# PEER experts' two rows in one table row: one 8 KB gather for each pick, product and sum in one pass

## The chip, the cores and the metric

The kernel runs on one core of a Trainium2 chip. The metric is the device time of one execution in microseconds (us). The engines are named as in the profile: PE (TensorE), DVE (VectorE), ACT (ScalarE), POOL (GpSimd) and SP (the queue that issues plain transfers).

## The reference

One decoder block on 1024 tokens of width 1024, in float32: a mixer (attention over a sliding window, a short convolution, a projection), a layer norm, and then a channel mixer with 16,384 experts of one neuron each, on which the change bears:

```python
v1, i1 = lax.top_k(s1, 16)            # 8 heads, two halves of a product key
v2, i2 = lax.top_k(s2, 16)
cand = v1[..., :, None] + v2[..., None, :]
sc, pos = lax.top_k(cand, 16)         # 16 experts for each head
e = i1[pos // 16] * 128 + i2[pos % 16]
g = softmax(sc)
# 8 * 16 = 128 picks for each token
u = u_experts[e]; v = v_experts[e]    # rows of 1024 floats
a = gelu(einsum('tkd,td->tk', u, x))
out = einsum('tk,tkd->td', g * a, v)
```

The block ends with `layer_norm(ALPHA * h + out)`.

## The kernel before

The 1024 tokens are eight blocks of 128, a block's tokens on the 128 partitions. The channel mixer is computed in two ways. For blocks 2 to 5 (`DENSE`) every expert is computed by matmuls: `up` (L677 to L690) loads 128 experts' u rows, splits them into two float32r parts (`uh` on ACT, `ul` on DVE, L120 and L121), multiplies on PE (L684), applies Gelu and the gates (`ge`, L689 and L690) and splits the result (`Wh`, `Wl`); `down` loads the v rows, splits them (`vh` on ACT, `vl` on POOL), multiplies (L716) and adds into `accT` on DVE (L722). There are 128 calls of each: the 256 units of the dense stage. For blocks 0, 1, 6 and 7 (`ROWS`) the rows of the picked experts are gathered: `gathered` (L139) makes 128 steps over the u table and then 128 over the v table. A u step issues an indirect DMA on POOL (L148), 128 rows of 4 KB into a tile `row`, and DVE multiplies it by the tokens' rows and sums along the row (L150). After 128 of them one Gelu (L152) and one product with the gates (L153) give the weights `a`. A v step gathers (L160), and DVE adds `row * a[:, k]` to the accumulator `acc` (L162). The tokens' rows (`h1p`) and the accumulator lie in the one PSUM tile `pg`, in turn; the gathered rows, the copies of the tokens' rows and the parameters of the second norm share five 4 KB slots (`t4k`, `NGATHER = 5`).

The steps come out of one generator. `advance_rows` takes three of them (one from `c = 26` on) behind each projection of the first stage, and `advance` (L749) takes as many behind each dense unit as brings all 1024 to their end at nine tenths of the 256 units:

```python
goal = min(total, early + AHEAD + (total - early - AHEAD) * u * 10 // (9 * units))
for _ in range(goal - done):
    step()
```

The order in which each engine gets its instructions is not the program's: a planner simulates the timeline when the kernel is built and puts an instruction into its engine's queue when its operands and its buffer are ready by its estimate. Each queue then runs in that order.

The first stage goes through the tokens in four groups of two blocks: projections (`project`, L370), attention, convolution, output projection, norm, keys and the choice of experts. A generator `side` runs the choice of the preceding group beside it; for dense blocks it also builds the gates (`gates_of_all`, L261 to L275). The tiles `x`, `y` and `h` of 8 KB share the tag `T`, with four buffers.

Of the kernel before, what the change touches and what calls it, by code (L numbers as in the profile page):

```python
# [13 lines left out]
F32 = mybir.dt.float32  # L14
# [40 lines left out]
NGATHER = 5  # L55
TK = 4
# [21 lines left out]
def block_kernel(ctx: ExitStack, tc: tile.TileContext, d, out):  # L78
# [49 lines left out]

    def second_norm(tb, src):
        par = []  # L130
        for i in (2, 3):
            p = gp.tile([P, D], F32, name="ln2", tag="t4k", bufs=NGATHER)
            G.dma_start(p, ln2d[:, i:i + 1].to_broadcast([P, 1, D]).rearrange("p a e -> p (a e)"))
            par.append(p)
        o = gp.tile([P, D], F32, name="o", tag="t4k", bufs=NGATHER)
        layer_norm(o, src, par, gp)
        G.dma_start(out[tb * P:(tb + 1) * P], o)

    def gathered(tb):  # L139
        g = gw[tb].rearrange("p h k -> p (h k)")  # L140
        h1 = gp.tile([P, D], F32, name="h1", tag="t4k", bufs=NGATHER)
        G.dma_start(h1, h1d[tb])
        h1p = pg.tile([P, D], F32, name="pg")
        act(h1p, h1, AF.Copy)
        a = gp.tile([P, P], F32, name="a", bufs=2)
        for k in range(P):
            row = gp.tile([P, D], F32, name="row", tag="t4k", bufs=NGATHER)
            G.indirect_dma_start(out=row, out_offset=None, in_=d["u"],  # L148
                                 in_offset=bass.IndirectOffsetOnAxis(ap=idx[tb][:, k:k + 1], axis=0))
            V.scalar_tensor_tensor(row, row, 1.0, h1p, op0=ALU.mult, op1=ALU.mult, accum_out=a[:, k:k + 1])  # L150
            yield True
        act(a, a, AF.Gelu)  # L152
        V.tensor_tensor(a, a, g, op=ALU.mult)  # L153
        acc = pg.tile([P, D], F32, name="pg")
        h1 = gp.tile([P, D], F32, name="h1", tag="t4k", bufs=NGATHER)
        G.dma_start(h1, h1d[tb])
        act(acc, h1, AF.Copy, scale=ALPHA)
        for k in range(P):
            row = gp.tile([P, D], F32, name="row", tag="t4k", bufs=NGATHER)
            G.indirect_dma_start(out=row, out_offset=None, in_=d["v"],  # L160
                                 in_offset=bass.IndirectOffsetOnAxis(ap=idx[tb][:, k:k + 1], axis=0))
            V.scalar_tensor_tensor(acc, row, a[:, k:k + 1], acc, op0=ALU.mult, op1=ALU.add)  # L162
            yield True
# [616 lines left out]
def lay_out(i):  # L780
    def m(name):
        return np.asarray(i[name])
# [32 lines left out]
```

## Time and profile before

| | |
|---|---|
| Time of three runs, median (lowest to highest) | 2746.32 us (2743.99 to 2756.95) |
| The profiled execution | 2743.4 us, span 2741.6 us |
| Busy: PE, DVE, ACT, POOL | 84%, 84%, 29%, 52% |
| Gathers | 1024 indirect DMAs from POOL |
| Moved | 862.21 MB, 314 GB/s over the span |

The span is the time from the first instruction to the last; the 1.8 us between it and the execution's time lie around it. A share of busy time is a mean over stages that differ: the first stage runs to about 1225 us, the dense stage to about 2612 us, and what is left runs to the end. Which engine a stage waits for is read from that stage alone.

### The profile page before, as it was taken

The page shows a single profiled execution, that of the slowest core. Times are in us where ns is not written, and L with a number is a line of the kernel's source. Part 1 is how long each engine was busy: PE and PEld are TensorE (multiplying, and loading weights), DVE is VectorE, ACT ScalarE, POOL GpSimd, SP SyncE. Part 2 cuts the span into 40 slices and gives each one's busy share as a digit, 9 for nine tenths or more (in the row PEclk, how much of TensorE's full clock was granted, in tenths as well). Part 3 has the DMA queues.
Part 4 walks back from the last instruction along what each step waited for, and adds up shares of the span by engine and source line. Part 5 has one row for each costly group of instructions (what it writes and reads, how often), then busy time and mean ns, then how long its engine had stood idle before and what let it go on. Part 6 is the DMA issues. An engine that isn't in the chain of part 4 may idle for free. (4 is left out here: it accounts for less than half of the span.)

```text
span 2741.6 us, 33269 instructions
## 1 busy us (share of the span) xinstructions
PE 2290.9 (84%) x11032; PEld 1917.8 (70%) x11032; DVE 2303.3 (84%) x4956; ACT 798.1 (29%) x1307; POOL 1415.2 (52%) x1233
## 2 busy tenths in 40 slices
PE   8999699789887622219999999999999999999940
PEld 7888587678766522218888888888888888888830
DVE  2158889999999999978888888888888888888897
ACT  2123122242443323224232322323232332323201
POOL 1000533443353344436667676666767666666753
PEclk9899799799977755559999999999999999999975
DMA  6355999899979788899999999999999999999987
GB/s 203 99 155 175 347 376 332 311 336 354 337 286 337 253 317 293 309 337 322 343 337 340 336 352 350 341 351 335 342 354 334 347 344 346 339 342 353 335 314 263
DMA packets 293900, 862.21 MB, mean 314 GB/s; under 512 B 25824, under 2 KB 97760, under 8 KB 289504
## 3 DMA queue, kind: packets, MB, share of 16 engines
q0 software_dynamic: 150480, 548.47, 54.5%
q1 hardware_dynamic: 143248, 311.62, 33.1%
q8 instruction: 87, 1.43, 0.2%
q14 instruction: 85, 0.70, 0.1%
HBM read 815.95 MB, written 44.04 MB: 314 GB/s over the span
## 5 line engine op out<-in xcount | busy, mean ns | idle before, releaser
L148 POOL DMA_INDIRECT row<-in_u,ix x512 | 532.9, 1041 | 586.7 <-DVE row L150 242.9
L160 POOL DMA_INDIRECT row<-in_v,ix x512 | 554.8, 1084 | 474.4 <-DVE pg L162 229.9
L162 DVE SCALAR_TENSOR_TENSOR pg<-row,a,pg 128x1024 f32<-128x1024 f32 x512 | 656.4, 1282 | 33.8 <-DMA row<-in_v,ix 27.8
L684 PE MATMUL pd<-hT,uh 128*128 128x512 f32 x2048 | 635.8, 390 | 42.8 <-ACT uh L120 42.8
L150 DVE SCALAR_TENSOR_TENSOR row<-row,pg 128x1024 f32<-128x1024 f32 x512 | 611.7, 1212 | 45.4 <-DMA row<-in_u,ix 44.8
L684 PEld LDWEIGHTS pd<-hT,uh 128*128 128x128 f32 x2048 | 385.4, 188 | 123.0 <-ACT uh L120 43.0
L716 PE MATMUL pd<-Wl,vh 128*128 128x512 f32 (+1 forms) x1056 | 402.3, 383 | 0.0
L684 PE MATMUL pd<-hT,ul 128*128 128x512 f32 x1024 | 399.3, 390 | 0.0
L716 PE MATMUL pd<-Wh,vh 128*128 128x512 f32 (+1 forms) x1056 | 397.4, 383 | 0.2 <-ACT Wh L120 0.2
L716 PE MATMUL pd<-Wh,vl 128*128 128x512 f32 (+1 forms) x1056 | 392.1, 383 | 0.3 <-POOL vl L121 0.3
L121 POOL TENSOR_TENSOR vl<-vraw,vh 128x1024 fp32r<-128x1024 f32 x128 | 309.4, 2417 | 72.7 <-ACT vh L120 68.6
L267 PE MATMUL pk<-o,oh 128*128 128x128 f16 x512 | 109.2, 277 | 208.2 <-DVE oh L261 131.3
L370 PE MATMUL mm<-x,raw 128*128 128x256 f32 x1152 | 269.2, 386 | 13.1 <-DMA x<-in_xT 7.7
L120 ACT ACTIVATE vh<-vraw 128x1024 fp32r<-128x1024 f32 x128 | 135.9, 1062 | 455.7 <-PE pd L716 302.1
L722 DVE TENSOR_TENSOR accT<-accT,pd 128x512 f32<-128x512 f32 (+1 forms) x256 | 169.4, 667 | 109.8 <-PE pd L716 97.8
L370 PEld LDWEIGHTS mm<-x,raw 128*128 128x128 f32 x1152 | 215.8, 193 | 45.2 <-issue 8.1
L370 PE MATMUL mm<-h,raw 128*128 128x256 f32 x1024 | 238.1, 385 | 1.5 <-ACT h L539 1.0
L716 PEld LDWEIGHTS pd<-Wh,vl 128*128 128x128 f32 x1056 | 198.4, 188 | 39.3 <-POOL vl L121 0.7
L716 PEld LDWEIGHTS pd<-Wl,vh 128*128 128x128 f32 x1056 | 198.5, 188 | 38.9 <-DVE Wl L121 0.2
L716 PEld LDWEIGHTS pd<-Wh,vh 128*128 128x128 f32 x1056 | 198.0, 188 | 39.2 <-ACT Wh L120 0.4
L121 DVE TENSOR_TENSOR ul<-uraw,uh 128x1024 fp32r<-128x1024 f32 x128 | 159.7, 1248 | 76.1 <-ACT uh L120 70.8
L684 PEld LDWEIGHTS pd<-hT,ul 128*128 128x128 f32 x1024 | 192.8, 188 | 40.9 <-DVE ul L121 0.8
(211 smaller groups left out, 2756.0 us busy)
## 6 DMA issues: line engine op xcount, KB each, us to landing
raw<-in_wall SPq DMA_DIRECT2D x168, 512.0 KB
uraw<-in_uT SPq DMA_DIRECT2D x128, 512.0 KB
vraw<-in_vL SPq DMA_DIRECT2D x128, 512.0 KB
gd<-st SPq DMA_DIRECT2D x32, 1024.0 KB
gq<-gd SPq DMA_DIRECT2D x32, 1024.0 KB
row<-in_u,ix POOLq DMA_INDIRECT x512
row<-in_v,ix POOLq DMA_INDIRECT x512
x<-in_xT SPq DMA_DIRECT2D x16, 256.0 KB
```

The lines of the kernel that those rows point to most:

```text
L120: act(dh, src, AF.Copy)
L121: eng.tensor_tensor(dl, src, dh.bitcast(F32), op=ALU.subtract)
L148: G.indirect_dma_start(out=row, out_offset=None, in_=d["u"], in_offset=bass.IndirectOffsetOnAxis(ap=idx[tb][:, k:k + 1], axis=0))
L150: V.scalar_tensor_tensor(row, row, 1.0, h1p, op0=ALU.mult, op1=ALU.mult, accum_out=a[:, k:k + 1])
L160: G.indirect_dma_start(out=row, out_offset=None, in_=d["v"], in_offset=bass.IndirectOffsetOnAxis(ap=idx[tb][:, k:k + 1], axis=0))
L162: V.scalar_tensor_tensor(acc, row, a[:, k:k + 1], acc, op0=ALU.mult, op1=ALU.add)
L267: nc.tensor.matmul(ps[:, t], oh[:, :, t2 + t], o1[:, t2 + t], start=True, stop=False)
L370: nc.tensor.matmul(ps[:, :n], w[:, j], mov[:, j, :n], start=(j == 0), stop=(j == NJ - 1))
L684: nc.tensor.matmul(ps, w[:, j], hT[z][:, j], start=(j == 0 and k == 0), stop=(j == NJ - 1 and k == 2))
L716: nc.tensor.matmul(ps, vv[:, j % 2, k], w[:, t0:t0 + n], start=(k == 0 and p == 0), stop=(k == QUAD - 1 and p == 2))
L722: V.tensor_tensor(o, o, ps, op=ALU.add)
```

## The change

The host puts the u row and the v row of an expert side by side into one table `uv`, so that a row has 8 KB. `gathered` makes one gather for each pick into a pair tile `[P, 2, D]`, of which there are five (tag `uv`). DVE forms the product of pick k in the first half; two ACT instructions on one column of `a` apply Gelu and the gate; behind the product of pick k stands the sum of pick k - 1, from the second half of its pair. The number of steps is still 1024. The tokens' rows stay in SBUF (`h1`, a tile of its own) and are an operand of the product from there; `pg` holds the accumulator alone. The second norm takes its two parameters with one DMA into a pair. Room is made by three buffers instead of four for the tag `T`, and by setting `dynamic_dma_scratch_size` to 8192.

```diff
 NGATHER = 5
+SCRATCH = 8192
...
+    def pair(name):
+        return gp.tile([P, 2, D], F32, name=name, tag="uv", bufs=NGATHER)
+
     def second_norm(tb, src):
-        par = []
-        for i in (2, 3):
-            p = gp.tile([P, D], F32, name="ln2", tag="t4k", bufs=NGATHER)
-            G.dma_start(p, ln2d[:, i:i + 1].to_broadcast([P, 1, D]).rearrange("p a e -> p (a e)"))
-            par.append(p)
-        o = gp.tile([P, D], F32, name="o", tag="t4k", bufs=NGATHER)
-        layer_norm(o, src, par, gp)
+        par = pair("ln2")
+        G.dma_start(par, ln2d[:, 2:4].to_broadcast([P, 2, D]))
+        o = pair("o")[:, 0]
+        layer_norm(o, src, (par[:, 0], par[:, 1]), gp)
         G.dma_start(out[tb * P:(tb + 1) * P], o)
 
     def gathered(tb):
...
-        h1 = gp.tile([P, D], F32, name="h1", tag="t4k", bufs=NGATHER)
+        h1 = gp.tile([P, D], F32, name="h1")
         G.dma_start(h1, h1d[tb])
-        h1p = pg.tile([P, D], F32, name="pg")
-        act(h1p, h1, AF.Copy)
+        acc = pg.tile([P, D], F32, name="pg")
+        act(acc, h1, AF.Copy, scale=ALPHA)
         a = gp.tile([P, P], F32, name="a", bufs=2)
-        for k in range(P):
-            row = gp.tile([P, D], F32, name="row", tag="t4k", bufs=NGATHER)
-            G.indirect_dma_start(out=row, out_offset=None, in_=d["u"],
-                                 in_offset=bass.IndirectOffsetOnAxis(ap=idx[tb][:, k:k + 1], axis=0))
-            V.scalar_tensor_tensor(row, row, 1.0, h1p, op0=ALU.mult, op1=ALU.mult, accum_out=a[:, k:k + 1])
-            yield True
-        act(a, a, AF.Gelu)
-        V.tensor_tensor(a, a, g, op=ALU.mult)
-        acc = pg.tile([P, D], F32, name="pg")
-        h1 = gp.tile([P, D], F32, name="h1", tag="t4k", bufs=NGATHER)
-        G.dma_start(h1, h1d[tb])
-        act(acc, h1, AF.Copy, scale=ALPHA)
-        for k in range(P):
-            row = gp.tile([P, D], F32, name="row", tag="t4k", bufs=NGATHER)
-            G.indirect_dma_start(out=row, out_offset=None, in_=d["v"],
-                                 in_offset=bass.IndirectOffsetOnAxis(ap=idx[tb][:, k:k + 1], axis=0))
-            V.scalar_tensor_tensor(acc, row, a[:, k:k + 1], acc, op0=ALU.mult, op1=ALU.add)
-            yield True
+        rows = {}
+        for k in range(P + 1):
+            if k < P:
+                rows[k] = pair("row")
+                G.indirect_dma_start(out=rows[k].rearrange("p a e -> p (a e)"), out_offset=None, in_=d["uv"],
+                                     in_offset=bass.IndirectOffsetOnAxis(ap=idx[tb][:, k:k + 1], axis=0))
+                ru = rows[k][:, 0]
+                V.scalar_tensor_tensor(ru, ru, 1.0, h1, op0=ALU.mult, op1=ALU.mult, accum_out=a[:, k:k + 1])
+                act(a[:, k:k + 1], a[:, k:k + 1], AF.Gelu)
+                act(a[:, k:k + 1], a[:, k:k + 1], AF.Copy, scale=g[:, k:k + 1])
+                yield True
+            if k:
+                V.scalar_tensor_tensor(acc, rows.pop(k - 1)[:, 1], a[:, k - 1:k], acc, op0=ALU.mult, op1=ALU.add)
+                yield True
         second_norm(tb, acc)
...
-            x = p2.tile([P, NJ, NM], F32, name="x", tag="T", bufs=4)
+            x = p2.tile([P, NJ, NM], F32, name="x", tag="T", bufs=3)
...
-        "u": f(m("u_experts")[0]),
-        "v": f(m("v_experts")[0]),
+        "uv": f(np.concatenate([m("u_experts")[0], m("v_experts")[0]], axis=1)),
...
-    nc = bacc.Bacc("TRN2", target_bir_lowering=False, num_devices=1)
+    nc = bacc.Bacc("TRN2", target_bir_lowering=False, num_devices=1, dynamic_dma_scratch_size=SCRATCH)
```

The tiles `h` and `y` get `bufs=3` likewise, and the last norm's parameters come from `pair("ln2")[:, 0]`.

## Rows read from the trace of the kernel before

**Rows 1.** The page's span in 40 equal slices, busy tenths, two of its lines

```profile
PE   8999699789887622219999999999999999999940
...
DMA  6355999899979788899999999999999999999987
```

**Rows 2.** Windows: stretch, length, PE, PEld, DVE, ACT, POOL busy; PEclk, DMA share, GB/s

```profile
300.00:400.00 100.00, 93.52 (x455) 82.00 (x454) 83.02 (x252) 20.04 (x44) 45.04 (x48) 0.91 1.00 381
...
1225.00:2612.50 1387.50, 1381.34 (x6107) 1143.80 (x6108) 1173.41 (x1474) 433.07 (x540) 936.11 (x712) 1.00 0.95 342
300.00:1225.00 925.00, 620.37 (x3438) 524.75 (x3436) 873.28 (x2631) 282.64 (x567) 394.57 (x378) 0.77 0.89 323
```

**Rows 3.** Windows of the products (L150) alone, then of the sums (L162) alone, DVE busy

```profile
0.00:1225.00 1225.00, 308.09 (x512) 0.81 0.80 286
1225.00:2612.50 1387.50, 306.79 (x512) 1.00 0.95 342
...
1225.00:2612.50 1387.50, 408.32 (x318) 1.00 0.95 342
2612.50:2715.00 102.50, 82.18 (x64) 0.61 0.92 324
```

**Rows 4.** DVE's waits from 1225 to 2612.5: total us, times, longest

```profile
DVE accT L722 <- PE pd L716: 97.6, 127, 2.2
DVE ul L121 <- ACT uh L120: 70.8, 71, 9.0
...
DVE ge L690 <- ACT ge L689: 0.8, 2, 0.5
```

**Rows 5.** DVE's waits from 300 to 1225, the longest first

```profile
DVE row L150 <- DMA row<-in_u,ix: 32.6, 37, 3.0
...
DVE a L153 <- ACT a L152: 0.4, 1, 0.4
```

**Rows 6.** The page's costliest groups of instructions: the two gathers on POOL

```profile
L148 POOL DMA_INDIRECT row<-in_u,ix x512 | 532.9, 1041 | 586.7 <-DVE row L150 242.9
L160 POOL DMA_INDIRECT row<-in_v,ix x512 | 554.8, 1084 | 474.4 <-DVE pg L162 229.9
```

**Rows 7.** The page's DMA queues: packets, MB, packets' time as share of 16 engines

```profile
q0 software_dynamic: 150480, 548.47, 54.5%
q1 hardware_dynamic: 143248, 311.62, 33.1%
```

**Rows 8.** Timeline of DVE, 1643 to 1646: start us, us, instruction

```profile
1643.20 1.23 DVE L121 TENSOR_TENSOR ul<-uraw,uh 128x1024 fp32r<-128x1024 f32 x1 [1.87 <-ACT uh L120]
1644.34 1.22 DVE L150 SCALAR_TENSOR_TENSOR row<-row,pg 128x1024 f32<-128x1024 f32 x1
1645.48 0.08 DVE L150 DVE_READ_ACCUMULATOR row<-row,pg 128x1 f32 x1
```

**Rows 9.** ACT's groups by form: small activations and table loads

```profile
L109 ACT ACT_TABLE_LOAD x8 | 10.3, 1283 | 0.1
L109 ACT ACTIVATE lnst<-lnst 128x1 f32<-128x1 f32 x16 | 3.0, 200 | 4.0 <-DVE lnst L108 3.9
...
L452 ACT ACTIVATE S<-sp,nm 128x128 f32<-128x128 f32 x8 | 2.8, 366 | 2.6 <-DVE nm L448 2.6
```

**Rows 10.** Timeline of DVE and POOL from 2600 to 2604

```profile
2600.84 2.41 POOL L121 TENSOR_TENSOR vl<-vraw,vh 128x1024 fp32r<-128x1024 f32 x1
...
2601.13 2.69 DVE L690 TENSOR_TENSOR ge<-ge,gq 128x512 f32<-128x512 f32 x1
```

**Rows 11.** Groups by form from 1225 to 2612: the splits and the gating

```profile
L121 POOL TENSOR_TENSOR vl<-vraw,vh 128x1024 fp32r<-128x1024 f32 x128 | 309.4, 2417 | 72.7 <-ACT vh L120 68.6 <-issue 2.7
...
L121 DVE TENSOR_TENSOR ul<-uraw,uh 128x1024 fp32r<-128x1024 f32 x128 | 159.7, 1248 | 76.1 <-ACT uh L120 70.8 <-issue 3.0 <-PE pd L684 1.8
...
L690 DVE TENSOR_TENSOR ge<-ge,gq 128x512 f32<-128x512 f32 x128 | 92.0, 718 | 0.8 <-ACT ge L689 0.8
```

**Rows 12.** ACT's waits from 1260 to 2600, two of the longest

```profile
ACT vh L120 <- PE pd L716: 302.1, 91, 6.6
...
ACT vh L120 <- DMA vraw<-in_vL: 108.4, 20, 8.7
```

More of the change, by code (lines that the diff above doesn't have):

```diff
@@ L530, in normed @@
             blocks, nb, n, t0 = spans(gi)
-            h_ = p2.tile([P, NJ, NM], F32, name="h", tag="T", bufs=4)
+            h_ = p2.tile([P, NJ, NM], F32, name="h", tag="T", bufs=3)
             for b, tb in enumerate(blocks):
@@ L639, in block_kernel @@
             x, qkv = xin
-            y = p2.tile([P, NJ, NM], F32, name="y", tag="T", bufs=4)
+            y = p2.tile([P, NJ, NM], F32, name="y", tag="T", bufs=3)
             for b in range(2):
@@ L769, in block_kernel @@
         for i in (2, 3):
-            p = gp.tile([P, D], F32, name="ln2", tag="t4k", bufs=NGATHER)
+            p = pair("ln2")[:, 0]
             nc.sync.dma_start(p, ln2d[:, i:i + 1].to_broadcast([P, 1, D]).rearrange("p a e -> p (a e)"))
```

## The prediction

> **What bounds the kernel now.** I read the page's slices first, to cut the span into stages, then windows of each stage, the waits of DVE and ACT in each, and the timeline where one stage hands over to the next. In the slices the reader is to see three stretches [rows 1]: PE and DMA uneven in the first 18 slices, both at nine tenths or more in the next 20, and in the last two PE gone and DMA still at work.
>
> From 300 to 1225 us DVE is busy 873 of 925 us, and PE 620 [rows 2]: here every us of DVE counts, and so does every wait of it. The largest of those is that of the products for their gather, 32.6 us in 37 waits [rows 5]; in the 100 us behind 300, where the steps come three behind each projection, the DMA share is 1.00 at 381 GB/s [rows 2].
>
> From 1225 to 2612.5 us PE is busy 1381 of 1387.5 us at full clock [rows 2], so this stage can't get shorter by anything done to the gathers. DVE has 1387.5 - 1173.4 = 214 us idle, most of it behind PE and ACT [rows 4], and the DMA share is 0.95 at 342 GB/s.
>
> At 2612.5 us PE has nothing of weight left, but 64 sums of the last block are still to come, and they take until 2715 us: 1.60 us each, of which DVE works 1.28, with the DMA engines busy 0.92 of the time [rows 3]. This tail of 102.5 us and the last norms behind it are on the path. By 1225 us 256 products and 130 sums are done; 256 products and 382 sums follow [rows 3]. So the kernel is worth what stage one's DVE, and the tail, are worth.
>
> **The change, part by part.** *Gathers.* 512 of 1024 gathers go, with 512 x 1.06 = 544 us of POOL [rows 6]. POOL is at 936 of 1387 us in the dense stage and under half before it [rows 2], and its gathers wait for DVE to free a row longer than for anything else [rows 6]: no time comes from this directly. Were an 8 KB gather to cost POOL twice a 4 KB one, nothing would be lost either.
>
> *Bytes and packets.* The bytes stay. Page part 3 gives 16 x 2741.6 us x 0.545 / 150480 = 0.159 us for a packet of 3645 bytes on the gathers' queue, and 0.101 us for one of 2175 bytes on the other [rows 7]. A line through both is an estimate: 0.016 us for a packet and 0.039 us for a KB of 1000 bytes. Two rows of 4 KB then take 0.353 us and one of 8 KB 0.337, 4.6% less. Bounds: nothing, if a row is cut in two, and 4.6%.
>
> *Bytes in flight.* Five slots of 4 KB with one in use leave four gathers, 16 KB for a partition, in flight; five pairs, with the one being multiplied and the one waiting for its sum in use, leave three, 24 KB. Each is asked for some six steps ahead instead of four. That is what the 32.6 us of product waits can be cured by: bounds 0 and 32.6; I take half, **-16 us**, since where the DMA share is already 1.00 depth alone doesn't help.
>
> *The tail.* Sixty-four sums become 32 picks of the same bytes. With 4.6% off the packets it takes 97.8 us, and with the share going from 0.92 to 1.00, as it stands where three steps follow each projection [rows 2], 90: **-12 us**. Bounds: 0, and -25 where DVE ends last (64 steps at 1.21 us, the mean of a product, 1.14 us start to start [rows 8], and a sum, 1.28).
>
> *Steps moved out of the tail.* The dense stage could take more steps: DVE has 214 us idle, and from 0.95 to 0.97 of DMA share there are 10 MB, 19 gathers of 0.524 MB. Whether the planner puts them there depends on when it thinks that a pair lands, which no row shows; in the trace DVE waits little for gathers in this stage, so the plan is later than the data. Bounds: none, and all 64 (-90 us: 77 us of DVE, and 366 GB/s). Nearer to the first: half of those 19, at 1.41 us each, **-13 us**.
>
> *DVE's own work.* The product's second operand moves from PSUM to SBUF. `ul`, two operands of the same size in SBUF, lasts 1.23 us, and the next instruction starts 1.14 us behind its start; the product lasts 1.22 and is followed after 1.14 [rows 8]. No difference. What reading SBUF twice can cost beside POOL stands below as a rival; in the forecast it lies in DVE's 214 us.
>
> *ACT.* 1024 instructions on one column are added, 0.20 us each by the one-column square root [rows 9]: 205 us on an engine at 283 of 925 and 433 of 1387 us [rows 2]. A chain of product, Gelu, scaling and sum is new. Two such instructions take 0.4 us, and at least one product (1.14 us) lies between, so the sum finds `a` ready where ACT is free. ACT's queue is in order, and an instruction of attention or a split may stand ahead and wait; DVE's waits for ACT's small results are next to nothing so far, 0.8 us in the dense stage and 0.4 in stage one [rows 4, 5]. Gelu now comes up in stage one, among Exp and Sqrt, each of which then loads its table again, 1.28 us [rows 9]: the attention of three groups has 12 quartets of Exp, and the sinks, gates and norms some 12 places more; at one or two loads each these make 30 to 60 us of ACT, of which I let DVE feel **+8 us** (bounds 0 and 40).
>
> *The rest.* Gelu and gates of a whole block, the second copy and load of the tokens' rows, and one of two parameter loads go; they are few, and beside other work. The third buffer for `x`, `y`, `h` is asked for when its old tenant has been read a stage earlier, so the lost fourth costs nothing; if a load of `x` waits after all, it is three times some us. The smaller descriptor store is not visible in any row: taken as nothing, and if POOL waits for room, its idle time covers it.
>
> Sum, against the profiled execution's own 2743.4 us: 2743.4 - 16 - 12 - 13 + 8 = **2710 us**. That execution is 2.9 us below the median of the three runs.
>
> **Rivals.** *POOL and DVE block each other* (slower). At 2601.13 us `ge`, with two operands in SBUF, took 2.69 us, where its mean is 0.72 [rows 11], while POOL's split `vl` of 2.41 us ran, and it ended behind it [rows 10]. The products and sums, with an operand in PSUM, show nothing of it: their means in the dense stage are 1.20 and 1.28 us [rows 3]. The new product has two in SBUF, and the splits fill 309 of 1387 us [rows 11]. For 319 products that start anywhere, 0.22 of them wait 1.2 us on average: 85 us, inside the 214. The old pairs meet more seldom than that (the mean of `ul` is 1.25 us [rows 11] beside the 1.23 of one that meets nothing [rows 8]). It decides when it passes 214 us, 0.67 us for each product; if each of 128 splits holds up DVE for its full length, it is 310 us, 96 too many, and `ge` and `ul` come late for PE: **2810 us** from 2710. The page "SBUF — State Buffer" of the Trainium skill, section "Who interferes with whom", says that a DVE instruction with two SBUF inputs contends with a GpSimd instruction that reads SBUF, one of them waiting out the other; by that rule the product pays as above, and the trace's `ge` agrees with 2.69 us.
>
> *The queues tie up* (slower). ACT waits up to 6.6 us for PE and up to 8.7 us for `vraw` [rows 12]. If a Gelu stands behind such a wait, the next sum holds up DVE, and with it `ge` for PE. Against it: DVE is the late one of the two. A wait of 0.3 us for each of 193 picks in stage one, where nothing covers it, is 58 us: **2770 us**. Weights that come later beside rows of twice the size end in the same place: those 108 us [rows 12] doubled, and half of the addition reaching PE, is 54 us.
>
> *Nothing moves.* Landing times are hidden already, the planner leaves the same 64 steps, and the DMA engines take 8 KB like two of 4: the terms -16 to -13 shrink to some -5 and +8 stands against them: **2746 us**.
>
> *The change does more than forecast.* All 64 steps go into the dense stage: **2640 us**.
>
> **Chances.** The forecast, with its own range of 2675 to 2732, has 0.46; all moved or most of it 0.08; nothing moves 0.20; the queues 0.14; POOL and DVE 0.12. Faster by over 0.5% (about what a measurement of this kernel can tell from no change, 14 us) is 0.54, within it 0.20, slower 0.26. The range is **2655 to 2795**: below it lies about half of the case in which all moves, above it half of the case of the port, a tenth together; the costs without a row (the planner's landing times, the tie of the queues) make it no narrower.
>
> **What would show it.** Right: 512 gathers; DVE's waits for them below 20 us before 1225; the dense stage's PE still at 99%; under 30 picks behind PE's last matmul, at under 2.85 us each. The product's mean stays below 1.4 us in the dense stage; above 1.9 the port decides. DVE's waits for ACT on `a` under 20 us; if they are the longest of its waits, the queues decide. The prediction fails if the first stage no longer ends near 1220 us or PE falls below 97% in the dense one.

## The result and the profile after

The changed kernel takes **2764.98 us** (median of seven runs, 2763.06 to 2768.86), the kernel before in the same session 2745.81 (2743.99 to 2756.95): ratio 1.0067, 95% interval 1.0052 to 1.0082. It is slower by some 19 us, where 2710 was forecast. The profiled span is 2762.9 us (2741.6 before).

The page of the changed kernel, lines that answer to [rows 1, 6, 7]:

```profile
PE   8999689778976922221999999999999999999996
...
DMA  6355999799877878789998988989998999999985
...
q0 software_dynamic: 75600, 546.34, 51.7%
...
L153 POOL DMA_INDIRECT row<-in_uv,ix x512 | 695.7, 1359 | 1418.8 <-DVE pg L161 867.7
```

Half the gathers, half the packets on their queue, nearly the same bytes: an 8 KB row is one packet and not two. The queue's share fell from 54.5 to 51.7%. PE's stretch of nines begins one slice later and now reaches the last slice: the tail is gone, and the first stage is longer. To see by how much, both traces are cut at the first matmul of the dense stage and at the end of the last one of `down` (windows as in [rows 2]; first the kernel before, then the changed one):

```profile
0.00:1231.00 1231.00, 889.77 (x4761) 754.77 (x4762) 1021.45 (x3338) 356.66 (x750) 421.04 (x459) 0.81 0.80 286
1231.00:2631.00 1400.00, 1399.47 (x6259) 1161.58 (x6259) 1191.27 (x1506) 432.01 (x539) 944.73 (x720) 1.00 0.95 341
2631.00:2742.00 111.00, 1.65 (x16) 1.41 (x13) 90.59 (x114) 9.47 (x18) 49.47 (x54) 0.52 0.81 293
```

```profile
0.00:1307.00 1307.00, 903.01 (x4760) 761.10 (x4760) 1082.79 (x3349) 490.99 (x1220) 307.30 (x288) 0.79 0.78 291
1307.00:2739.00 1432.00, 1413.25 (x6258) 1162.06 (x6259) 1365.96 (x1548) 548.04 (x1127) 726.62 (x424) 1.00 0.91 333
2739.00:2763.00 24.00, 1.75 (x17) 1.52 (x14) 19.13 (x55) 7.66 (x16) 0.55 (x1) 0.60 0.28 110
```

The first stage grew by 77 us, the dense stage by 31, the rest shrank by 87. In the dense stage DVE works 175 us more for nearly the same steps: the windows of product and sum alone count 437, 587 and 0 of them in the three stretches, where it was 386, 583 and 55. Where those 175 us are, the groups by form of the changed kernel show (1307 to 2739 us, as [rows 11]):

```profile
L156 DVE SCALAR_TENSOR_TENSOR row<-row,h 128x1024 f32<-128x1024 f32 x293 | 421.9, 1442 | 0.0
L161 DVE SCALAR_TENSOR_TENSOR pg<-row,a,pg 128x1024 f32<-128x1024 f32 x294 | 377.6, 1284 | 30.6 <-ACT a L158 30.2
L122 DVE TENSOR_TENSOR ul<-uraw,uh 128x1024 fp32r<-128x1024 f32 x128 | 225.4, 1761 | 39.3 <-ACT uh L121 39.1
...
L689 DVE TENSOR_TENSOR ge<-ge,gq 128x512 f32<-128x512 f32 x128 | 136.4, 1066 | 0.4 <-ACT ge L688 0.4
L122 DVE TENSOR_TENSOR Wl<-ge,Wh 128x512 fp32r<-128x512 f32 x128 | 105.3, 823 | 0.9 <-ACT Wh L121 0.9
```

The four with two operands in SBUF are slower, the sum, with one in PSUM, is not. `ul` had 1.25 us and `ge` 0.72 [rows 11]; the edit touches neither. What holds them up stands in the timeline, DVE and then POOL:

```profile
1653.88 3.81 DVE L156 SCALAR_TENSOR_TENSOR row<-row,h 128x1024 f32<-128x1024 f32 x1
1657.63 0.08 DVE L156 DVE_READ_ACCUMULATOR row<-row,h 128x1 f32 x1
...
1654.20 2.40 POOL L122 TENSOR_TENSOR vl<-vraw,vh 128x1024 fp32r<-128x1024 f32 x1
```

A product of 1.22 us takes 3.81, which is its own time, the whole 2.40 of POOL's split and 0.19 more. This is what the page "SBUF — State Buffer" of the Trainium skill, section "Who interferes with whom", says of a DVE instruction with two SBUF inputs beside a GpSimd instruction that reads SBUF; the trace agrees, with 2.6 us on one product.

DVE's waits of the changed kernel, first stage (300 to 1307 us) and dense stage (1307 to 2739), answer to [rows 4, 5]:

```profile
DVE oh L260 <- PE pk L266: 15.9, 5, 4.2
DVE row L156 <- DMA row<-in_uv,ix: 14.6, 16, 2.6
DVE pg L161 <- ACT a L158: 10.3, 21, 1.4
...
DVE ul L122 <- ACT uh L121: 39.1, 21, 12.3
DVE pg L161 <- ACT a L158: 30.2, 48, 1.2
DVE accT L721 <- PE pd L715: 3.6, 5, 1.0
```

DVE's 97.6 us of waiting for PE before have become 3.6. PE's waits in the dense stage, behind its first matmul, show the other side (1310 to 2739 us):

```profile
PE pd L683 <- DVE ul L122: 6.6, 7, 3.5
PE pd L715 <- DVE Wl L122: 4.8, 8, 0.9
...
PE pd L715 <- DVE accT L721: 1.6, 1, 1.6
```

Now PE waits for DVE, 13.0 us of 17.7 in all; in the kernel before, all its waits in the stage are 0.5 us.

### The profile page after: what moved, and what is told of

Read it like the earlier page. It is cut to its first block, busy times and chain, and to the rows that moved or that the text cites. A ratio compares the mean times of both kernels' runs of the same rounds, so it can differ in the third digit from the quotient of the medians.

```text
span 2762.9 us, 32900 instructions
## 1 busy us (share of the span) xinstructions
PE 2318.0 (84%) x11032; PEld 1924.7 (70%) x11032; DVE 2467.9 (89%) x4952; ACT 1046.7 (38%) x2361; POOL 1034.5 (37%) x713
## 3 DMA queue, kind: packets, MB, share of 16 engines
q0 software_dynamic: 75600, 546.34, 51.7%
## 4 chain that ended last, share of the span: by engine, by line
DVE 41%; PE 37%; issue 9%; DMA 7%; ACT 5%; POOL 1%; SPq 0%; DVEq 0%; ACTq 0%; POOLq 0%
PE pd L715 15%; PE pd L683 12%; DVE pg L161 11%; DVE row L156 10%; PE mm L369 7%; DMA row<-in_uv,ix 4%; DVE ul L122 3%; DVE ge L689 2%; DVE accT L721 2%; DMA gd<-st 2%; DVE Wl L122 1%; DVE scr L197 1%; DVE ol L260 1%; DVE o L255 1%; DMA uraw<-in_uT 1%
## 5 line engine op out<-in xcount | busy, mean ns | idle before, releaser
L153 POOL DMA_INDIRECT row<-in_uv,ix x512 | 695.7, 1359 | 1418.8 <-DVE pg L161 867.7
L156 DVE SCALAR_TENSOR_TENSOR row<-row,h 128x1024 f32<-128x1024 f32 x512 | 687.5, 1344 | 17.5 <-DMA row<-in_uv,ix 17.4
L157 ACT ACTIVATE a<-a 128x1 f32<-128x1 f32 x512 | 103.6, 202 | 946.8 <-DVE row L156 946.1
L122 POOL TENSOR_TENSOR vl<-vraw,vh 128x1024 fp32r<-128x1024 f32 x128 | 325.0, 2542 | 71.1 <-ACT vh L121 60.4
L369 PE MATMUL mm<-x,raw 128*128 128x256 f32 x1152 | 272.3, 391 | 10.3 <-DMA x<-in_xT 7.4
L122 DVE TENSOR_TENSOR ul<-uraw,uh 128x1024 fp32r<-128x1024 f32 x128 | 225.4, 1761 | 39.3 <-ACT uh L121 39.1
L369 PEld LDWEIGHTS mm<-h,raw 128*128 128x128 f32 x1024 | 193.1, 194 | 32.1 <-ACT cT L557 4.9
L270 ACT ACTIVATE st<-pk 128x256 f32<-128x256 f32 x256 | 137.1, 628 | 171.4 <-PE pk L267 130.0
```

The source lines that it names most:

```text
L122: eng.tensor_tensor(dl, src, dh.bitcast(F32), op=ALU.subtract)
L153: G.indirect_dma_start(out=rows[k].rearrange("p a e -> p (a e)"), out_offset=None, in_=d["uv"], in_offset=bass.IndirectOffsetOnAxis(ap=idx ...
L156: V.scalar_tensor_tensor(ru, ru, 1.0, h1, op0=ALU.mult, op1=ALU.mult, accum_out=a[:, k:k + 1])
L157: act(a[:, k:k + 1], a[:, k:k + 1], AF.Gelu)
L270: act(st[z][:, :, tt:tt + 4].rearrange("p n t -> p t n"), ps[:, :, z * 64:(z + 1) * 64], AF.Copy, scale=1.0 / GSCALE)
L369: nc.tensor.matmul(ps[:, :n], w[:, j], mov[:, j, :n], start=(j == 0), stop=(j == NJ - 1))
```

## Experiments

Theory 1: the product's second SBUF operand, and an order of the queues that puts POOL's split beside DVE's other two-SBUF work, make DVE late for PE; the steps only change places between tail and first stage. Rivals: the chain over ACT; the pairs and their bytes; the steps pulled into the first stage.

Stages are cut as above, from the profiled run of each kernel; the ratio is to the kernel before, on the same chip (2745.2 to 2749.7 us in those sessions). The first expectations, up to the two runs with `vh` late, cut the dense stage some 30 us shorter: their 1401 us of the changed kernel is 1432 here. "Excess" is the time by which product, `ul`, `ge` and `Wl` of the dense stage exceed count x 1.22, 1.22, 0.69 and 0.69 us, their means where no `vl` runs (first run below).

| Kernel | Median us | Ratio (95%) | First, dense, rest us | Excess us: product; others |
|---|---|---|---|---|
| before | 2745.8 | 1 | 1231, 1400, 111 | 0; 11 |
| changed | 2765.0 | 1.0067 (1.0052 to 1.0082) | 1307, 1432, 24 | 65; 134 |
| changed, no `vl` | 2735.8 | 0.9957 (0.9943 to 0.9970) | 1309, 1399, 25 | 0; 0 |
| before, no `vl` | 2743.8 | 0.9994 (0.9980 to 1.0007) | 1235, 1398, 109 | 0; 0 |
| before, SBUF operand | 2799.5 | 1.0203 (1.0186 to 1.0220) | 1250, 1440, 104 | 89; 29 |
| changed, `pd` 4 | 2772.4 | 1.0101 (1.0078 to 1.0125) | 1313, 1436, 23 | 74; 131 |
| the same, PSUM operand | 2768.5 | 1.0084 (1.0062 to 1.0105) | 1269, 1416, 83 | 0; 126 |
| changed, `vh` late | 2755.3 | 1.0023 (1.0012 to 1.0034) | 1310, 1431, 15 | 65; 53 |
| PSUM operand, `vh` late | 2783.9 | 1.0127 (1.0107 to 1.0147) | 1277, 1443, 66 | 0; 116 |
| changed, order of before | 2740.4 | 0.9982 (0.9971 to 0.9992) | 1305, 1410, 24 | 60; 29 |
| PSUM operand, order of before | 2762.8 | 1.0056 (1.0040 to 1.0073) | 1268, 1409, 83 | 0; 30 |
| changed, sum two behind | 2780.3 | 1.0111 (1.0087 to 1.0136) | 1308, 1450, 21 | 70; 156 |
| changed, hold at 386 | 2792.6 | 1.0155 (1.0133 to 1.0177) | 1263, 1435, 94 | 54; 151 |
| before, 10 slots | 2751.8 | 1.0020 (1.0010 to 1.0030) | 1271, 1466, 15 | 0; 106 |
| 10 slots, hold at 386 | 2746.0 | 1.0008 (0.9998 to 1.0017) | 1223, 1474, 48 | 0; 133 |
| 10 slots, hold at 410 | 2713.1 | 0.9890 (0.9874 to 0.9907) | 1231, 1458, 18 | 0; 119 |
| 10 slots, hold at 410, order of before | 2792.2 | 1.0159 (1.0137 to 1.0180) | 1231, 1536, 24 | 0; 130 |
| 10 slots, order of before | 2790.5 | 1.0153 (1.0133 to 1.0172) | 1268, 1506, 15 | 0; 119 |
| 7 slots, hold at 410 | 2694.2 | 0.9806 (0.9779 to 0.9833) | 1220, 1403, 65 | 0; 73 |
| 8 slots, hold at 410 | 2708.1 | 0.9856 (0.9829 to 0.9883) | 1238, 1402, 65 | 0; 86 |

The excess alone does not set the dense stage: with 73 us of excess (7 slots) the stage is 3 us longer than before, with 30 (PSUM operand, order of before) 9 us. PE's waits in the stage go with its length: 0.5 us in the kernel before, none without `vl`, 2.0 with 7 slots, 7.4 with that order, with or without the PSUM operand, 17.7 in the changed kernel.

**POOL's split taken away.** In `values_of`, of the changed kernel and of the kernel before; both leave out the low part of v:

```diff
-            vl = dn.tile([P, 2, QUAD, P], F32R, name="vl", tag=tags[1], bufs=2)
-            split(vh, vl, raw, G)
-            return vh, vl
+            act(vh, raw, AF.Copy)
+            return vh, vh
```

> The changed kernel without the low part of v: GpSimd's split of each quad of v (325 us in all) is left out and the high part is used in its place, so the output loses the low part of v. DVE's order of products, sums and splits is that of the changed kernel, PE's matmuls are the same in number. Theory 1 (the product with two SBUF operands, and with it DVE's other two-SBUF work, is held up by GpSimd's split; the 214 us of DVE's slack in the dense stage are eaten, PE is late by some 26 us): product's mean in the dense stage falls from 1.44 to about 1.21 us, ul from 1.76 to about 1.25, ge from 1.07 to about 0.7; the dense stage falls from 1401 to about 1375 us, total about 2735 to 2742. Rival (DVE waits behind the chain over ACT, or for gathers): means of the products stay, total within 5 us of the changed kernel, 2760 to 2770.

> The control: the kernel before with the same part left out (GpSimd's split of v; the output loses the low part of v). Its product has one operand in PSUM. Theory 1: product, ul and ge keep their means of 1.20, 1.25 and 0.72 us to within 0.05, and the total stays within 6 us of the kernel before. Rival (leaving the split out makes the dense stage faster by itself, whatever the product reads): the total falls by 20 us or more here too, as it does in the changed kernel.

The changed kernel's dense stage, groups by form without the split:

```profile
L156 DVE SCALAR_TENSOR_TENSOR row<-row,h 128x1024 f32<-128x1024 f32 x293 | 356.5, 1220 | 0.0
...
L122 DVE TENSOR_TENSOR ul<-uraw,uh 128x1024 fp32r<-128x1024 f32 x128 | 156.5, 1224 | 84.0 <-ACT uh L121 83.5
L689 DVE TENSOR_TENSOR ge<-ge,gq 128x512 f32<-128x512 f32 x128 | 88.1, 688 | 27.8 <-ACT ge L688 27.3
```

Every excess is gone, with as many steps in each stage as before the cut and DVE's queue in much the same order; the dense stage is 33 us shorter and the total 29 us, now under the kernel before. In the kernel before the same cut moves nothing that can be told. The waits of the sums for ACT are still 29 us: they don't make it slow. Nor do the gathers: DVE waits for none in the changed kernel's dense stage.

**The operand alone, in the kernel before.** No pairs, no chain over ACT; T has three buffers and the descriptor store 8192, for the room:

```diff
-        h1 = gp.tile([P, D], F32, name="h1", tag="t4k", bufs=NGATHER)
-        G.dma_start(h1, h1d[tb])
-        h1p = pg.tile([P, D], F32, name="pg")
-        act(h1p, h1, AF.Copy)
+        h1p = gp.tile([P, D], F32, name="h1p")
+        G.dma_start(h1p, h1d[tb])
```

> The kernel before with one part of the change alone: the product's second operand, the tokens' rows, stays in a tile in SBUF (room by three buffers of T and the smaller descriptor store). Gathers, Gelu and gates of a block, and DVE's order are those of before but for three steps. Theory 1 (a product with two SBUF operands waits out a vl; it costs time only where DVE has no slack): in the dense stage the product's mean rises from 1.20 to 1.4 to 1.7 us over 256 products, ul, ge and Wl rise too as far as DVE falls behind, the excess over the instructions' least times is 80 to 200 us beside 214 us of slack; PE's dense stage grows by 0 to 20 us, total 2745 to 2770. Rival (the collisions of the changed kernel come from its pairs and ACT's chain, not from the operand): product's mean stays under 1.3 us, total within 5 us of before.

Its products in the dense stage:

```profile
L148 DVE SCALAR_TENSOR_TENSOR row<-row,h1p 128x1024 f32<-128x1024 f32 x256 | 396.2, 1566 | 34.1 <-DMA row<-in_u,ix 33.6
```

The product's mean was foreseen (1.4 to 1.7 us), the total not: it rose by 54 us, more than twice the upper bound. The excess is 118 us beside 214 us of idle time, and yet PE's stage is 40 us longer: PE waits 14.0 us for POOL's `vl` and 9.5 for `ul` (0.3 and nothing before). So slack counted over a stage did not cover these hold-ups; how `vl` itself comes to be late was not taken apart. DVE's waits for gathers rise too, from 9 to 34 us for the products. The first stage is 19 us longer as well: the products wait 49.1 us for their gathers there (32.6 before); why is open.

**The operand back in PSUM, in the changed kernel,** for the dense stage, where two banks are free if `pd` has four buffers; and the control with four buffers alone:

```diff
-        pd = s2.enter_context(tc.tile_pool(name="pd", bufs=6, space=PS, reuse_waits="tile"))
+        pd = s2.enter_context(tc.tile_pool(name="pd", bufs=4, space=PS, reuse_waits="tile"))
+        late["ph"] = s2.enter_context(tc.tile_pool(name="ph", bufs=1, space=PS, reuse_waits="tile"))
...
+                if "ph" in late and hp is h1:
+                    hp = late["ph"].tile([P, D], F32, name="hp")
+                    act(hp, h1, AF.Copy)
-                V.scalar_tensor_tensor(ru, ru, 1.0, h1, op0=ALU.mult, op1=ALU.mult, accum_out=a[:, k:k + 1])
+                V.scalar_tensor_tensor(ru, ru, 1.0, hp, op0=ALU.mult, op1=ALU.mult, accum_out=a[:, k:k + 1])
```

> The changed kernel, but in the dense stage the product reads the tokens' rows from a copy in PSUM (two banks, taken from the buffers of the dense accumulators, six to four). As a consequence of the moved pool the planner places fewer steps ahead of the dense stage (196 products and 195 sums, where it was 219 and 218) and leaves 26 sums and 25 products behind PE's last weights. Theory 1: product's mean in the dense stage about 1.21 us, ul about 1.25, PE's dense stage about 1375 us; the first stage shorter by 46 steps x 1.25 = 58 us, of which the tail of 51 steps takes back 25 picks x 2.9 = 73 us minus the 10 that are there already: total about 2735 to 2755. Rival (the ACT chain, or the bytes, set the dense stage): the dense stage stays at about 1400 us, total 2765 or more.

> The control for the run with PSUM: the changed kernel with four buffers of the dense accumulators in place of six, and nothing else; DVE's order is that of the changed kernel. All theories: within 10 us of the changed kernel (2755 to 2775). If it is slower by more, the run with PSUM has to be read against this one and not against the changed kernel.

Products and `ul` in the dense stage:

```profile
L162 DVE SCALAR_TENSOR_TENSOR row<-row,hp 128x1024 f32<-128x1024 f32 x296 | 359.1, 1214 | 0.0
L122 DVE TENSOR_TENSOR ul<-uraw,uh 128x1024 fp32r<-128x1024 f32 x128 | 222.5, 1739 | 68.5 <-ACT uh L121 68.2
```

The product is free, and the dense stage is 20 us shorter than in the control; but `ul` is still held up, against the expectation. So the operand is one part of the cause. The total, 2768.5 us, missed Theory 1's 2735 to 2755 and lies where its rival had it (2765 or more), though the stage does not: the rival left it as long as in the control. 41 steps are left behind the dense stage (51 by the expectation's cut), which was foreseen; the hold-up of `ul` was not.

**The order of the splits.** Why `ul` at all? ACT's timeline gives the answer, the kernel before and then the changed one, a cycle of four ups and four downs:

```profile
1958.31 1.06 ACT L120 ACTIVATE uh<-uraw 128x1024 fp32r<-128x1024 f32 x1 [1.14 <-PE pd L684]
...
1963.85 1.06 ACT L120 ACTIVATE vh<-vraw 128x1024 fp32r<-128x1024 f32 x1 [0.76 <-PE pd L716]
1968.56 1.06 ACT L120 ACTIVATE vh<-vraw 128x1024 fp32r<-128x1024 f32 x1 [3.65 <-PE pd L716]
1976.12 1.06 ACT L120 ACTIVATE vh<-vraw 128x1024 fp32r<-128x1024 f32 x1 [6.50 <-DMA vraw<-in_vL]
1981.02 1.06 ACT L120 ACTIVATE vh<-vraw 128x1024 fp32r<-128x1024 f32 x1 [3.85 <-PE pd L716]
1984.83 1.06 ACT L120 ACTIVATE uh<-uraw 128x1024 fp32r<-128x1024 f32 x1 [2.74 <-PE pd L684]
```

```profile
1940.83 1.04 ACT L121 ACTIVATE uh<-uraw 128x1024 fp32r<-128x1024 f32 x1
...
1944.55 1.05 ACT L121 ACTIVATE vh<-vraw 128x1024 fp32r<-128x1024 f32 x1
...
1945.92 1.05 ACT L121 ACTIVATE vh<-vraw 128x1024 fp32r<-128x1024 f32 x1
1946.87 1.04 ACT L121 ACTIVATE uh<-uraw 128x1024 fp32r<-128x1024 f32 x1
...
1963.19 1.04 ACT L121 ACTIVATE uh<-uraw 128x1024 fp32r<-128x1024 f32 x1
1964.14 1.05 ACT L121 ACTIVATE vh<-vraw 128x1024 fp32r<-128x1024 f32 x1
1965.09 1.04 ACT L121 ACTIVATE uh<-uraw 128x1024 fp32r<-128x1024 f32 x1
```

Before, the four `vh`, and with them POOL's `vl`, stand in one run, while PE works through the downs and DVE does `accT` and steps, all with an operand in PSUM; in ACT's queue it is so in 31 of 32 cycles. After, the planner has strewn them among the ups, and `vl` runs beside `ul`, `ge` and `Wl`. No line of the diff does that. Two edits try to put it back. The first holds each `vh` behind the last `Wh` of its quad:

```diff
-            split(vh, vl, raw, G)
+            with tc.issue_after(whi[q * QUAD + QUAD - 1].ins):
+                act(vh, raw, AF.Copy)
+            G.tensor_tensor(vl, raw, vh.bitcast(F32), op=ALU.subtract)
```

`whi` holds ACT's instructions that write `Wh`.

> The changed kernel, but ACT's vh of a quad (and by it POOL's vl) is held behind the last Wh of the same quad, as ACT's queue had it in the kernel before. Nothing is left out. In the changed kernel half of the vl run beside the next ups; 111 of 124 vl hold up a DVE instruction, 204 us in all, 139 of it on ul, ge and Wl; before it was 5 of 128 and 8 us. Theory 1a (the order put vl beside DVE's two-SBUF work of the ups): ul's mean falls from 1.76 to under 1.35, ge's from 1.07 to under 0.8 us, the product's stays at 1.4 us or rises, DVE's excess falls to some 80 us, which fits into its slack; the dense stage loses 15 to 25 us, total 2740 to 2752. Theory 1b (DVE falls behind because of the products' own collisions, and ul, ge and Wl are pushed beside vl only by that): ul and ge stay above 1.5 and 0.9 us, total above 2755.

> The two edits together: in the dense stage the product reads the tokens' rows from PSUM, and vh and vl stand behind the last Wh of their quad. Theory 1: no DVE instruction is held up (product 1.21, ul 1.25, ge 0.72 us), PE is busy over 99% of the dense stage, which takes 1375 us; 21 products and 22 sums are left for the tail, at 2.9 us a pick; total 2750 to 2760, 10 to 15 us under the run with PSUM alone. Rival (something else makes PE late in the dense stage, the gathers' bytes or the ACT chain): the dense stage stays above 1390 us, total within 5 us of the run with PSUM alone.

`ul` falls to 1.24 us, but `ge` only from 1.07 to 0.95, and PE now waits for `vl` itself, 10.6 us in 20 waits in the stage and 22.4 with the PSUM operand. The stage does not get shorter (1431 us, and 1443 with the PSUM operand); 9 us are gained behind it. It was the wrong place: Theory 1's total was missed by 3 us in the first run and by 24 in the second. The first just reaches the total of Theory 1b, above 2755, but not its mean of `ul`, above 1.5; the second lies 15 us above the run with PSUM alone, where neither theory had it. The second edit restores the order as it was, with the `uh` of two ups traced ahead (`parts`) and the `vh` of a cycle in one run behind them (`parts` and `values_of` also hold each `uh` and `vh` behind the one that is to come before it):

```diff
+            if jj == 2 and q < last:
+                parts(4 * q + 5)
+                parts(4 * q + 6)
-            v = values_of(q, jj)
+            v = ahead.pop(jj, None) or values_of(q, jj)
...
+            if jj == 3 and q + 1 < last:
+                ahead[0] = values_of(q + 1, 0)
+                ahead[1] = values_of(q + 1, 1)
```

> The changed kernel with the order of the splits as it was before: the four vh of a cycle in one run on ACT, behind the uh of two ups ahead. Nothing is left out. Theory 1 (the planner strewed the splits): ul, ge and Wl are held up by under 25 us instead of 139, the product by 60 to 110; DVE's slack covers most of it. How much of a burst it covers is open: in the run with the operand alone 114 us of excess in this order made the dense stage 40 us longer, so from 1400 to 1430 us for the stage; total 2735 to 2762. Rival (the pairs' depth or ACT's chain): ul, ge and Wl are still held up by over 80 us.

> The changed kernel with the order of the splits as before and the tokens' rows in PSUM for the dense stage's products: both parts of the contention away, the pairs, the depth and ACT's chain kept. Theory 1: excess of all DVE instructions under 25 us, PE idle under 6 us, the dense stage 1400 to 1406 us; with the first stage at 1268 and the tail of 51 steps at 83 us, as in the run with PSUM alone, total 2750 to 2758. Rival (pairs or ACT's chain make PE late): dense stage above 1412, total above 2764.

`ul` and `ge` with the order restored, the products still reading SBUF:

```profile
L158 DVE SCALAR_TENSOR_TENSOR row<-row,h 128x1024 f32<-128x1024 f32 x293 | 417.8, 1426 | 0.0
...
L686 DVE TENSOR_TENSOR ul<-uraw,uh 128x1024 fp32r<-128x1024 f32 x128 | 160.5, 1254 | 66.3 <-ACT uh L685 66.2
L706 DVE TENSOR_TENSOR ge<-ge,gq 128x512 f32<-128x512 f32 x128 | 102.0, 797 | 12.5 <-ACT ge L705 12.5
```

The others' excess falls from 134 to 29 us (under 25 was expected, over 80 by the rival), the dense stage from 1432 to 1410, the total by 25 us, to 2740.4: a little under the kernel before. With the PSUM operand in addition the excess is 30 us, but the stage stays at 1409 and the total 5 us above what was expected. So the two parts don't add up: the operand alone takes 20 us from the stage of its control, the order alone 22 from that of the changed kernel, both together 27 from the control's 1436, and what the last 9 us are was not found.

**The chain over ACT.** The sum two picks behind:

```diff
-            if k:
-                V.scalar_tensor_tensor(acc, rows.pop(k - 1)[:, 1], a[:, k - 1:k], acc, op0=ALU.mult, op1=ALU.add)
+            if k > 1:
+                V.scalar_tensor_tensor(acc, rows.pop(k - 2)[:, 1], a[:, k - 2:k - 1], acc, op0=ALU.mult, op1=ALU.add)
```

> The changed kernel with the sum two picks behind the product instead of one. In the changed kernel the sums wait 41 us for their weight from ACT, 10 of them in the first stage and 30 in the dense one. Theory 1 (the ACT chain is a small part): these waits fall below 8 us, and of 41 us the first stage gives 10 and the dense stage, where DVE is late for PE, up to 15; one pair less is in flight, for which the gather waits of the products may rise by 10 us; total 2745 to 2765. Rival (ACT's queue is what made the change slow): total at or below 2740.

The sums' wait in its dense stage:

```profile
DVE pg L161 <- ACT a L158: 30.2, 48, 1.6
```

It is what it was, and the kernel is 15 us slower. Both expectations fell: the wait does not come from the distance between product and sum. What it does come from was not taken apart.

**The steps in the first stage.** The gathers of steps from the 386th on are held behind the first split of the dense stage:

```diff
+                with tc.issue_after(late["mark"].ins) if done >= PIN and "mark" in late else nullcontext():
+                    G.indirect_dma_start(out=rows[k].rearrange("p a e -> p (a e)"), out_offset=None, in_=d["uv"],
...
+            if c == 0:
+                late["mark"] = G.tensor_copy(gp.tile([P, 1], F32, name="mark"), uh[:, 0, 0:1].bitcast(F32))
```

> The changed kernel with the gathers of steps from the 386th on held behind the first split of the dense stage, so that 388 steps instead of 437 are done ahead of it, as many as before; 29 products and 29 sums are left for the tail, and the dense stage has the same 578. Theory 1 (pulling steps into the first stage and taking them from the tail is an even trade, about 1.4 us a step either way): the dense stage begins about 65 us earlier, near 1240, the tail is 70 us longer, total 2755 to 2775. Rival (the steps pulled ahead are themselves the loss, since the first stage is bound by DVE and the tail is not): total 2700 to 2735.

The windows of its first stage and of what follows the dense stage, in which 49 steps are left:

```profile
0.00:1263.00 1263.00, 902.00 (x4760) 761.28 (x4760) 1027.01 (x3275) 479.14 (x1171) 261.91 (x259) 0.81 0.75 277
...
2699.00:2793.00 94.00, 1.50 (x14) 1.26 (x12) 78.59 (x133) 21.90 (x68) 31.81 (x23) 0.52 0.77 292
```

The first stage gives back 44 us for 49 steps, the tail takes 70 for them. So the trade is not even: a step pulled ahead cost 0.9 us and saved 1.4, and both expectations fell. The window shows a second thing: with 388 steps, two more than before, the first stage ends at 1263 and not at 1231. DVE's work in it is the same (1027 against 1021 us), its idle time 26 us longer. Of the 77 us, 32 belong to the rest of the change and not to the steps. 9 us are sums waiting for ACT; what the pairs and the SBUF operand each have in it was not taken apart (the operand alone, above, lengthened this stage by 19). The room that was made is not it: ten slots, below, with the same three buffers and descriptor store, end the stage at 1223 with 386 steps.

**Depth without pairs.** The kernel before with more 4 KB slots, with and without the hold; here too T has three buffers and the descriptor store 8192, for the room:

```diff
-NGATHER = 5
+NGATHER = 10
```

> The kernel before with ten 4 KB slots for its gathers in place of five: the bytes of the changed kernel's five pairs, with single rows, the product's operand in PSUM, no chain over ACT. 436 steps are placed ahead of the dense stage (386 before, 437 in the changed kernel), 588 in it, none is left for the tail. Theory 1 (the depth alone moves the steps; the rest of the change only costs): the first stage grows by 45 to 75 us, the tail loses 85 to 95, the dense stage stays at 1400 with ul, ge and the products unhindered; total 2715 to 2740. Rival (the pulled steps make the first stage longer by more than the tail gives back): 2750 or more.

> Ten 4 KB slots, and the gathers of steps from the 386th on held behind the first split of the dense stage: 386 steps ahead of it as before, 609 in it (574 before), 29 left for the tail. Theory 1 (only the dense stage has DVE time to give: 214 us): the first stage ends as before near 1231, the dense stage stays near 1400 to 1405 (35 steps more are 43 us of DVE), the tail falls from 64 to 29 sums of 1.6 us, 56 us; total 2685 to 2700. Rival (DMA can't carry 18 MB more in the dense stage, at 0.95 of its time busy): the dense stage grows by 20 us or more, total above 2710.

> As the run before with the hold from the 410th step on: 410 steps ahead of the dense stage, 607 in it, 7 left for the tail. Theory 1: the first stage grows by 20 to 30 us (24 steps at 0.9 to 1.3 us), the tail falls by 57 sums of 1.6 us, 91 us; total 2680 to 2695. If a step placed in the first stage costs what one in the tail does (1.6 us), it equals the run with the hold at 386 or lies 3 us under it.

> Ten 4 KB slots, the hold at the 410th step, and the order of the splits as before. Theory 1: the dense stage falls from 1458 to 1400 to 1410 us (ul, ge and Wl unhindered, PE's waits for vl and vh, 32 us, gone), the first stage stays near 1231, 8 sums are left: total 2655 to 2675. Rival (the depth makes the gathers in POOL's queue hold up vl, whatever ACT's order): PE still waits over 20 us for vl, total above 2695.

> Ten 4 KB slots without a hold, with the order of the splits as before: 436 steps ahead, none left. Theory 1: the dense stage falls from 1466 to 1400 to 1412 us, total 2685 to 2705, against 2752 without the order. Rival as in the run before: total above 2735.

Ten slots move the steps as five pairs do: 436 ahead, no tail. But the dense stage is 65 us longer, and with the order of before put back 106; the hold at 410 gains 38 us, the one at 386 six. All five totals miss what Theory 1 expected by 12 us or more, and those of four lie where their rivals had them. DVE's waits for gathers in the stage are under 8 us in each of the five, so the rival of the second run (DMA can't carry the bytes) is not borne out by them. PE's waits in it, with the hold at 410, from 1240 us to the stage's end, without and with the order:

```profile
PE pd L723 <- POOL vl L122: 23.9, 26, 1.9
PE pd L723 <- ACT vh L121: 8.3, 7, 1.2
```

```profile
PE pd L704 <- DVE ul L690: 60.9, 25, 3.9
PE pd L738 <- POOL vl L725: 9.5, 11, 4.6
```

It waits for the splits either way, and the theory of the order does not hold there: `ul`, `ge` and `Wl` lose 106 to 133 us in these kernels, though the four `vh` stand in one run in 25 to 28 of 32 cycles as the planner has them and in 31 with the edit. By the traces `vl` begins 2.1 to 2.6 us behind the end of its `vh` on the mean, where it was 0.5 in the kernel before, and runs beside `ul` for 42 to 62 us, where it was 3. So ACT's order alone does not keep them apart. That the gathers ahead of `vl` in POOL's queue delay it, the rival of the last two, was not tested; PE's wait for `vl`, 9.5 us, is less than the 20 that it named. Two more sizes, to tell depth from order:

> The kernel before with seven 4 KB slots and the gathers of steps from the 410th on held behind the first split of the dense stage: 410 steps ahead, 576 in the dense stage, 38 left for the tail; ACT's splits in the order of before. If the order of the splits sets the dense stage: 1400 to 1408 us for it, the first stage near 1231, the tail 18 + 38 x 1.6 = 70 to 80 us, total 2700 to 2715. If the depth itself does: the dense stage lies between 1400 and 1458, near 1420, total near 2725.

> The same with eight slots: the same 410, 576 and 38 steps; ACT's splits partly strewn as in the changed kernel (the first of a cycle one up later in 11 of 32, the second in 30). If the order sets the dense stage: longer than with seven slots by 5 to 20 us, total 2710 to 2735. If the depth does: near 1435, total near 2740.

Seven slots with the hold at 410:

```profile
0.00:1220.00 1220.00, 890.11 (x4761) 755.68 (x4761) 1044.32 (x3357) 354.99 (x750) 447.15 (x479) 0.81 0.83 297
1220.00:2622.00 1402.00, 1399.75 (x6254) 1160.70 (x6255) 1239.71 (x1513) 428.86 (x540) 971.68 (x730) 1.00 0.95 343
2622.00:2688.00 66.00, 2.22 (x20) 1.98 (x19) 57.65 (x88) 9.47 (x18) 23.75 (x27) 0.54 0.70 271
```

Seven and eight leave the dense stage at 1402 us, 6 and 2 us in total under what the order let expect, and the strewn splits of eight do not lengthen it, against the expectation of 5 to 20 us; nor do those of seven, whose four `vh` stand in one run in only 14 of 32 cycles and whose `vl` runs beside `ul` for 66 us. PE waits 2.0 and 1.1 us there. Something tips between eight and ten, and what it is stays open. Eight lie 14 us behind seven, by a first stage that is 18 us longer. Seven slots with the hold are the best version run: 2694.2 us, 1.9% under the kernel before. Seven without the hold, and the hold with five pairs in the order of before, were not run, so depth and hold are not told apart.

## Why the prediction was wrong

**The step that failed** is "What reading SBUF twice can cost beside POOL stands below as a rival; in the forecast it lies in DVE's 214 us". The mechanism of the rival was the right one, and both of its numbers were not. It counted the products, 85 us: they lost 65. It left the old ones at "meet more seldom than that": `ul`, `ge` and `Wl` lost 134, because the planner moved `vl` beside them. The sum, 199 us, is under the 214 that were to decide, and the dense stage grew by 31: the idle time of the stage does not cover them, and PE waits 13.0 us for DVE. Shown by the run without `vl`, which takes 29 us back and 33 of the stage, by the PSUM operand (20 us of the stage) and by the order alone (25 us in all). The sign that was named, the product's mean, read 1.44 us, between the 1.4 and the 1.9 that were to tell the cases apart: it looked at the smaller part.

**Steps moved out of the tail** (-13, and -12 for a faster tail) is the second step that failed. The tail went almost entirely, 87 us, more than forecast; but only four steps more went into the dense stage. The text asked only whether the planner would put them there; it put 51 into the first stage, which took back 77 of the 87 us, 44 of them for the steps as the run with the hold shows. The sign "no longer ends near 1220" came true with that, at 1307. The tail was also cut too early: from 2612.5 us, where PE was said to have nothing of weight left, to 2631 it is busy 18.47 of 18.50 us, so the tail was 84 us with 55 sums, not 102.5 with 64.

**Bytes in flight** (-16). The products' waits for gathers in the first stage fell from 32.6 to 14.6 us, by 18, as forecast. The stage did not gain it: the sums' waits for `a` take 10.3, and DVE's idle time in the stage is 224 us where it was 210. With seven single slots these waits fall to 7.4 us, and the stage is 11 us shorter with 24 steps more.

**ACT** (+8). Table loads rose from 21 to 59, and the sums wait 41 us, twice the 20 that were named as the bound; 30 of it lie in the dense stage, where the run without `vl` is no slower for it. The 10.3 us in the first stage are near the 8 that were let in. That this stage is 32 us longer with the steps held to the old number has no term in the sum.

**Gathers, bytes and packets** came as written, in size of no weight, and so did the room taken from T and the descriptor store.

So without POOL's split the change is worth -10 us (0.9957), where -33 had been forecast; with it, +19. Either error alone would have left a change of less than the 14 us that the prediction took as the least to be told (-33 + 29 is -4, and -10); the two together made it slower.

## What to carry to other kernels

When an operand moves from PSUM to SBUF, list every instruction on GpSimd that reads SBUF and every DVE instruction with two SBUF operands, not the moved one alone, and ask which of them the new queue order puts side by side; idle time summed over a stage is no cover, and PE's waits, not the sum of the hold-ups, say what the stage loses. When a planner orders the queues, compare the order of the unchanged instructions on each engine before costing anything: here it moved 51 steps into the first stage and the four splits of a cycle apart. Where only depth was wanted, more slots of the old size, with a hold on the steps pulled ahead, gave more than any version of the merged row that was run, up to a size that has to be measured.

## What the hardware showed unexpectedly

It is DVE that pays most. POOL's 128 `vl` of the changed kernel last 2.54 us on the mean, where it was 2.42, 16 us in all, while DVE lost 199. Beginning first, by the profile's marks, did not protect an instruction of DVE: the product at 1653.88 us had begun 0.3 us ahead of the split and still waited it out, and of the 48 of DVE's two-SBUF instructions that began 0.25 to 0.75 us ahead of a split, 22 were over 0.5 us longer than their mean without `vl`. A gather of 8 KB rows costs POOL 1.36 us, not the double of 1.06 [rows 6], and its rows travel as one packet each: the 66,176 packets of 8192 bytes on the queue took 0.341 us on the mean, where 0.337 was estimated, and two of 4096 bytes took 0.355 (0.178 each, in the kernel before).
